# adaLN rows in the recurrent loop of a two-layer diffusion trunk: VectorE accumulation, or column groups on TensorE

## The chip, the cores and the metric

The kernel runs on one core of a Trainium2 chip. The engines of the core work side by side, each through its own queue in order: TensorE (PE; matmuls, with weight loads listed apart as PEld), VectorE (DVE), ScalarE (ACT), GpSimd (POOL) and SyncE (SP), which here issues the DMAs. The metric is the device time of one execution in microseconds.

## The reference

Two layers over 256 tokens of width 2048, float32. Each layer has a token mixer and a SwiGLU feed-forward, each behind an adaLN shift and scale and in front of a gated residual with LayerNorm. The first layer's mixer is a bidirectional gated linear recurrence (RG-LRU) over 2816 channels, started from 256 context tokens; the second is a pooling mixer.

```python
for i in range(DEPTH):
    m = jnp.split((cond_lat @ mod_w[i] + mod_b[i])[:, None, :], 6, axis=-1)
    h = x * (1 + m[1]) + m[0]
    ...
    y = mix(h)            # layer 0: RG-LRU, layer 1: pooling
    x = _layer_norm(ALPHA * x + m[2] * y, ln_g[i, 0], ln_b[i, 0])
    h = x * (1 + m[4]) + m[3]
    x = _layer_norm(ALPHA * x + m[5] * _swiglu(h, ffn_w1[i], ffn_w3[i], ffn_w2[i]), ln_g[i, 1], ln_b[i, 1])
```

In the recurrence, `a = exp(-8 r softplus(-lam))` and `b = sqrt(1 - a^2) * (i * xb)` with `r` and `i` sigmoids of block-diagonal products of `xb`, the output of a short convolution over `h @ w_x`. The state runs `h_t = a_t h_(t-1) + b_t` in both directions; the sum of both is multiplied by `gelu(h @ w_gate)` and projected by `w_out`.

What the change is about is `cond_lat @ mod_w[i]`: one row of 2048 numbers times a 2048 x 12288 matrix, in six vectors of 2048 for each layer, 16.8 MB of weights for each vector.

## The kernel before

**Weights.** All matrices stream from HBM once. A float32 weight piece (`raw`, four buffers) is split into a high half `hi` (a cast to the fast matmul format) and a low half `lo = raw - hi` (`split_w`, lines 183 to 192), and each product is three matmuls (`mm3`, lines 214 to 217): high x high, and the two mixed ones. The cast runs on ScalarE, or on GpSimd where `hi_pool` is set; the difference on VectorE, or on GpSimd where `lo_pool` is set. Buffers of `hi` and `lo` are three each.

**Jobs.** The program is a list of jobs. A `Runner` writes them out: loads go ahead as far as the limits of their class allow (`raw` 4, `mraw` 2), splits go up to two weight jobs ahead, uses (the matmuls) in order. `spread_mod` interleaves a second list, the adaLN jobs, into a main list. A scheduler then orders the instructions on each engine by dependence and by the place in this program.

**Stages.** In the first stage the shift and scale of layer 0 are computed while half of `h @ w_x` already runs; here the adaLN rows (`mu`, line 416) are multiplied on TensorE, 32 columns wide in four column groups. Then comes the recurrent loop over eight pairs of blocks (352 channels each). For each pair `p`:

- `wx_job`: `w_x` of the pair, two k-tiles a job, three jobs for the first five pairs (the rest of their sums was made in the first stage), eight for the last three; results in banks 0 to 2.
- `gates(p - 1, 1)`: two jobs of the `r` and `i` products of the pair before, backward direction, in banks 3 to 5; sigmoids on ScalarE.
- `conv(p)`: the convolution taps on VectorE, put at the head of the background list `bg`.
- `gate_job`: eight jobs of `h @ w_gate` with the tokens stationary, 352 columns wide, in banks 6 and 7, closed by a gelu (`gtok`, line 573).
- `gates(p, 0)`: two jobs, forward direction, then `recur`.

`recur` (line 619) queues the recurrence: tanh on ScalarE and `i * xb` on GpSimd at once (`f1`), then in the background exp (`f2`), square root (`f3`), two products on VectorE (`f4`), and the scans on VectorE (`f5`). After the loop come the projection by `w_out`, the first feed-forward, the pooling mixer, and the second feed-forward.

**adaLN on VectorE.** `mod_jobs` (line 220) takes half a vector at a time: 16 loads of 128 rows x 1024 columns (`mraw`), each followed by one VectorE instruction, `acc = mraw * cond + acc` (lines 246 and 249, 243 behind a fence). GpSimd then cuts the accumulator in two (lines 274 and 275), TensorE sums over the partitions by a matmul with ones (284 and 285), and the vector is brought into columns by way of DRAM (`finish_cols`) or added to a broadcast row (`finish_row`). Seven halves stand in the recurrent loop, 112 such instructions (vectors 3 and 4 of layer 0, half of vector 0 of layer 1, and vector 2 of layer 0, whose accumulators are kept until `row_now`); eleven halves run beside the projection and the first feed-forward, and two beside the second.

**GpSimd in the loop.** It makes the high half of six of each pair's eight `gate_job` pieces (`GH`) and of all `gates` pieces, the low half of four of the eight (`GL`), and `i * xb`. Later it adds the position embedding, makes the low halves of transposed activations (`jit`, line 766), and scales rows.

Of the kernel before, what the change touches and what calls it, by code (L numbers as in the profile page):

```python
# [10 lines left out]
F32 = mybir.dt.float32  # L11
F32R = mybir.dt.float32r
AF = mybir.ActivationFunctionType
ALU = mybir.AluOpType
# [18 lines left out]
LD = 0.85  # L33
# [5 lines left out]
GH = (1, 1, 1, 0)  # L39
GL = (0, 1, 0, 1)  # L40
# [21 lines left out]
class Runner:  # L62
    """Weights stream through SBUF in the order in which TensorE uses them."""
# [76 lines left out]
def trunk(es, tc, x, ctxlat, cols_in, ccols, mod_w, mod_b, ln_g, ln_b, ffn_w1, ffn_w3, ffn_w2,  # L140
# [23 lines left out]
    nc.scalar.activation(cond, craw[:, 0:KT], AF.Silu)  # L164
    mb01 = P.tile([128, 2, KT], F32, name="mb01")
# [4 lines left out]
    R = Runner({"raw": 4, "mraw": 2, "mu": 8, "xc": 2})  # L170
# [49 lines left out]
    def mod_jobs(vectors):  # L220
        """Products of the rows of mod_w with the conditioning vector, half a vector at a
        time; the sums over the partitions of one half run beside the next half's rows."""
        js = []
        wait = []
        for layer, which, finish, *halves in vectors:
            for h in halves or range(2):
# [31 lines left out]
                if finish is None:  # L258
                    st["acc", h] = acc
                else:  # L260
                    for n in range(1024 // MW):
                        wait += sums(layer, which, 1024 // MW * h + n, acc, n, finish)
# [47 lines left out]
    def row_now(layer, which):  # L310
        row = st["rows"].tile([128, D], F32, name="rowm", bufs=2)
        nc.sync.dma_start(row, mod_b[layer:layer + 1, which * D:(which + 1) * D].broadcast_to((128, D)))
        st["row", layer, which] = row
        for n in range(4):
            b = bk[st["rowbanks"][n % 2]]
            acc = st["acc", n // 2][0]
            nc.tensor.matmul(b, ones, acc[:, n % 2 * 512:(n % 2 + 1) * 512], start=True, stop=True)
            finish_row(layer, which, n, b, 512)

# [20 lines left out]
    cm = S_pool.tile([128, KT, 32], F32, name="cm")  # L340
# [33 lines left out]
    # startup: shift and scale of the first layer, two k-tiles at a time  # L374
# [184 lines left out]
    def gate_job(p, kt):  # L559
# [17 lines left out]
        return wjob(two_kt(rg_w_gate, kt * 128, p * PW, PW), 128, 2 * PW, use, hi_pool=GH[kt // 2 % 4], lo_pool=GL[kt // 2 % 4])  # L577
# [12 lines left out]
    def gates(p, d):  # L590
        def use(mat, j):
# [5 lines left out]
            for o, parts in enumerate((((0, 128, 0), (256, 128, 1)),  # L597
# [3 lines left out]
                b = bk[3 + o]  # L601
# [12 lines left out]
        for mat in range(2):  # L614
            js.append(wjob([(lambda r: r[:, :832], rg_wri[mat, d, p])], 128, 832,
                           lambda j, mat=mat: use(mat, j), hi_pool=True))
        return js

    def recur(p, d):
# [5 lines left out]
        def f1(t):  # L625
# [4 lines left out]
            nc.gpsimd.tensor_tensor(i[t][:m], i[t][:m], xb[t][:m], op=ALU.mult)  # L630
# [14 lines left out]
        def f5(t):  # L645
# [7 lines left out]
            else:  # L653
# [6 lines left out]
                z = st["pair"].tile([128, 256], F32, name="yg", bufs=3)  # L660
                nc.vector.tensor_tensor(z[:m], y, q["g"][t][:m], op=ALU.mult)
                row = 0
                while row < m:
                    k, o = divmod(p * PW + t * 128 + row, 128)
                    n = min(128 - o, m - row)
                    nc.sync.dma_start(U[o:o + n, k * 256:(k + 1) * 256], z[row:row + n])
# [8 lines left out]
    VL = [(0, 3, finish_cols), (0, 4, finish_cols), (1, 0, finish_cols, 0)]  # L675
    VF = [(0, 5, finish_row), (1, 0, finish_cols, 1), (1, 1, finish_cols),
# [92 lines left out]
    def project(w, nk, source, banks, which, aux, final=False):  # L769
        """[tokens, D] product in three column passes: 0:1024, 1024:1536, 1536:2048."""  # L770
# [11 lines left out]
        def wide(k):  # L782
# [173 lines left out]
    # first layer: project the gated recurrence, then feed forward  # L956
# [179 lines left out]
def _columns(rows):  # L1136
    """Rows of 128 become columns."""
# [15 lines left out]
def _fold(rows):  # L1153
    """[n, 1024] becomes [128, 8, n]: channel 128 a + p at [p, a]."""
# [3 lines left out]
def _bands():  # L1158
    """Window means over the tokens, and the identity."""
# [12 lines left out]
def _gate_blocks(w):  # L1172
    """[2, 16, 176, 176] blocks as zero-padded tiles [2, 8, 128, 832]."""
# [46 lines left out]
```

## Time and profile before

| | |
|---|---|
| timed runs | 2616.08, 2622.93, 2627.61 us; median 2622.93 |
| profiled execution | span 2613.2 us from its first to its last instruction; its own time with what lies around that isn't listed |
| stretch 0 to 192 us | first stage |
| stretch 192 to 836 us | recurrent loop |
| stretch 836 to 1640 us | projection and first feed-forward |
| DMA over the span | 597.19 MB, mean 229 GB/s |

The span is 2.9 us below the fastest timed run and 9.7 below the median. A row of a group reads: line, engine, operation, output<-inputs, shapes, count, then busy us and mean ns of one, then idle time of the engine just before such instructions and what ended it. A row of a wait reads: engine and line that waited, <-, engine and line that released it: us in total, times, longest. A matmul's length in the timeline overlaps the next one's, so its cost is read from the distance between starts. The float32 matmuls of lines 416 and 434 appear as two records each. TensorE's granted clock is given as a share of full speed.

### The profile page before, as it was taken

To read this page: it belongs to the slowest core of one execution; us is meant where nothing else is said; L and a number is where in the kernel's file an instruction comes from. 1 tells how busy PE (TensorE), PEld (TensorE's weight loads), DVE (VectorE), ACT (ScalarE), POOL (GpSimd) and SP (SyncE) were. 2 spreads that over 40 slices of the span, in tenths; PEclk is the share of its full clock that TensorE was granted. 3 is DMA by queue.
4 is the path that set the end of the run, shared out by engine and by line. 5 is a ranking of instruction groups with operands and counts; after the bars stand their busy time and mean duration, and the time that the engine had idled before them with its cause. 6 is when DMAs were issued, how large, how long until landed. Compare 5 with 4: busy or idle time off the path is not lost.

```text
span 2613.2 us, 29167 instructions
## 1 busy us (share of the span) xinstructions
PE 2373.4 (91%) x10336; PEld 1879.9 (72%) x10336; DVE 1850.5 (71%) x1866; ACT 1166.8 (45%) x1465; POOL 805.2 (31%) x485
## 2 busy tenths in 40 slices
PE   8998788799887889999999998897899999999997
PEld 4557666677765668787877776675677888888885
DVE  3559999978887978877767778649866444444565
ACT  3215556545564444444434444445433444444453
POOL 0004555543354461100001134855410000003366
PEclk9999898899998989999999999998899999999999
DMA  9876565566675859899988888654587666666664
GB/s 311 266 218 217 168 181 164 171 213 214 190 244 188 284 208 325 308 308 314 306 304 312 289 285 266 194 151 148 196 295 254 192 188 191 186 192 186 186 196 135
DMA packets 287539, 597.19 MB, mean 229 GB/s; under 512 B 33160, under 2 KB 101768, under 8 KB 285344
## 3 DMA queue, kind: packets, MB, share of 16 engines
q1 hardware_dynamic: 287392, 595.32, 71.0%
q8 instruction: 81, 1.33, 0.2%
q14 instruction: 66, 0.54, 0.1%
HBM read 590.21 MB, written 2.15 MB: 227 GB/s over the span
## 4 chain that ended last, share of the span: by engine, by line
PE 49%; DVE 21%; DMA 18%; issue 7%; POOL 2%; ACT 2%; SPq 1%; DVEq 0%; POOLq 0%; ACTq 0%
DMA mraw<-in_mod_w 15%; PE bank L217 15%; PE bank L216 15%; PE bank L215 15%; DVE lo L191 7%; DVE acc L249 4%; PE bank L416 2%; DVE th L643 1%; DVE th L642 1%; DVE xb L543 1%; DMA raw<-in_rg_w_out 1%; DVE xt L750 1%; DVE y L652 1%; DVE xt L735 1%; POOL jit L766 1%
## 5 line engine op out<-in xcount | busy, mean ns | idle before, releaser
L191 DVE TENSOR_TENSOR lo<-raw,hi 128x1024 fp32r<-128x1024 f32 (+2 forms) x700 | 892.2, 1282 | 418.8 <-ACT hi L189 388.3
L189 ACT CAST hi<-raw 128x1024 fp32r<-128x1024 f32 (+1 forms) x660 | 672.1, 1020 | 960.5 <-PE bank L216 827.1
L217 PE MATMUL bank<-lo,hh 128*128 128x512 f32 x1440 | 567.5, 394 | 16.5 <-DVE lo L191 16.3
L249 DVE SCALAR_TENSOR_TENSOR acc<-mraw,cond,acc 128x1024 f32<-128x1024 f32 x300 | 425.2, 1417 | 212.7 <-DMA mraw<-in_mod_w 211.5
L215 PE MATMUL bank<-hi,hh 128*128 128x512 f32 x1440 | 567.6, 395 | 5.8 <-ACT hh L1059 4.3
L216 PE MATMUL bank<-hi,hl 128*128 128x512 f32 x1440 | 566.0, 393 | 3.6 <-DVE hl L856 2.7
L217 PE MATMUL bank<-lo,jit 128*128 128x512 f32 x880 | 352.2, 401 | 31.9 <-DVE lo L191 30.2
L216 PE MATMUL bank<-hi,jit 128*128 128x512 f32 x880 | 350.1, 398 | 10.9 <-POOL jit L766 10.9
L215 PE MATMUL bank<-hi,jit 128*128 128x512 f32 x880 | 347.3, 395 | 2.0 <-ACT hi L189 2.0
L766 POOL TENSOR_TENSOR jit<-gT,jit 128x512 fp32r<-128x512 f32 x132 | 236.0, 1790 | 352.5 <-ACT jit L765 352.5
L217 PEld LDWEIGHTS bank<-lo,hh 128*128 128x128 f32 x1440 | 272.9, 190 | 81.1 <-DVE lo L191 24.3
L216 PEld LDWEIGHTS bank<-hi,hl 128*128 128x128 f32 x1440 | 273.0, 190 | 62.8 <-DVE hl L856 4.1
L215 PEld LDWEIGHTS bank<-hi,hh 128*128 128x128 f32 x1440 | 273.0, 190 | 62.1 <-ACT hh L1059 4.8
L274 POOL TENSOR_SCALAR mh<-acc 128x512 fp32r<-128x512 f32 x36 | 34.2, 949 | 804.1 <-PE bank L284 600.2
L217 PEld LDWEIGHTS bank<-lo,jit 128*128 128x128 f32 x880 | 167.9, 191 | 78.5 <-DVE lo L191 41.8
L216 PEld LDWEIGHTS bank<-hi,jit 128*128 128x128 f32 x880 | 167.5, 190 | 51.8 <-POOL jit L766 13.9
L215 PEld LDWEIGHTS bank<-hi,jit 128*128 128x128 f32 x880 | 167.8, 191 | 39.7 <-ACT hi L189 3.3
L216 PE MATMUL bank<-hTh,lo 128*128 128x512 f32 (+1 forms) x384 | 153.2, 400 | 0.0
L215 PE MATMUL bank<-hTh,hi 128*128 128x512 f32 (+1 forms) x384 | 150.5, 405 | 1.8 <-ACT hTh L446 1.8
L217 PE MATMUL bank<-hTl,hi 128*128 128x512 f32 (+1 forms) x384 | 151.6, 396 | 0.0
L217 PE MATMUL bank<-lo,hTh 128*128 128x352 f32 x256 | 94.5, 370 | 49.3 <-DVE lo L191 37.7
L630 POOL TENSOR_TENSOR i<-i,xb 128x512 f32<-128x512 f32 (+1 forms) x48 | 97.0, 2037 | 127.4 <-ACT i L606 127.3
(153 smaller groups left out, 2835.4 us busy)
## 6 DMA issues: line engine op xcount, KB each, us to landing
raw<-in_ffn_w SPq DMA_DIRECT2D x528, 512.0 KB
mraw<-in_mod_w SPq DMA_DIRECT2D x320, 512.0 KB
mu<-in_mod_w SPq DMA_DIRECT2D x128, 256.0 KB
raw<-in_rg_w_x SPq DMA_DIRECT2D x64, 352.0 KB
raw<-in_rg_w_gate SPq DMA_DIRECT2D x64, 352.0 KB
raw<-in_rg_w_out SPq DMA_DIRECT2D x44, 512.0 KB
raw<-in_rg_wri SPq DMA_DIRECT2D x32, 416.0 KB
xc<-in_ctxlat SPq DMA_DIRECT2D x8, 512.0 KB
```

Of the source, the lines that this page charges most:

```text
L189: nc.scalar.copy(hi[:k, :n], raw[:k, :n])
L191: e.tensor_tensor(lo[:k, :n], raw[:k, :n], hi[:k, :n].bitcast(F32), op=ALU.subtract)
L215: nc.tensor.matmul(bank, lh, rh, start=start, stop=False)
L216: nc.tensor.matmul(bank, ll, rh, start=False, stop=False)
L217: nc.tensor.matmul(bank, lh, rl, start=False, stop=stop)
L249: nc.vector.scalar_tensor_tensor(a, raw, c, a, op0=ALU.mult, op1=ALU.add)
L274: nc.gpsimd.tensor_scalar(mh, a, 1.0, 0.0, op0=ALU.mult, op1=ALU.add)
L416: nc.tensor.matmul(bk[6][32 * g:32 * g + 32, :], cm[:, kk, :], j.raw[:, a].rearrange("p m f -> p (m f)"), start=kk < 4, stop=kk >= 12)
L543: nc.vector.scalar_tensor_tensor(o3[:, :, od], u3[:, :, us], rgcol(w, p, t)[:m], o3[:, :, od], op0=ALU.mult, op1=ALU.add)
L630: nc.gpsimd.tensor_tensor(i[t][:m], i[t][:m], xb[t][:m], op=ALU.mult)
L642: nc.vector.scalar_tensor_tensor(th[t][:m], r[t][:m], 1.0, th[t][:m], op0=ALU.add, op1=ALU.mult)
L766: nc.gpsimd.tensor_tensor(lo, src, hi.bitcast(F32), op=ALU.subtract)
```

## The change

In the recurrent loop the adaLN products use the way of the first stage. `mod_chunk` takes a quarter of a vector (512 columns) in eight pieces of 256 rows; two pieces give four matmuls, one for each of the four column groups, accumulated over the 16 k-tiles in bank 5. ScalarE copies the bank; four small matmuls with the selector `selt` then sum the groups and turn the result into columns, and VectorE adds the bias from the bank. For vector 2 of layer 0 the copies are kept, and `row_now` sums them with `selr`. Four whole vectors stand in the loop now, the second half of vector 0 of layer 1 among them, which leaves the later stage. The pieces use two buffers of `mraw` and the three of `jit`. All casts and low halves of the loop go to ScalarE and VectorE, and so does `i * xb`, which VectorE does in `f2`. Because bank 5 is taken, `gates` uses banks 3, 4, 0, 1 or 3, 4, 6, 7. The adaLN jobs are spread evenly over the loop, `yg` is written in place, and the conditioning tile `cm` moves to the base pool.

```diff
-LD = 0.85
-GH = (1, 1, 1, 0)
-GL = (0, 1, 0, 1)
...
+    selr = P.tile([128, 128], F32, name="selr")
+    nc.vector.tensor_scalar(selr, ones, selt[:, 0:1], None, op0=ALU.mult)
...
-    R = Runner({"raw": 4, "mraw": 2, "mu": 8, "xc": 2})
+    R = Runner({"raw": 4, "mraw": 2, "mu": 8, "xc": 2, "mp": 5})
...
-            acc = st["acc", n // 2][0]
-            nc.tensor.matmul(b, ones, acc[:, n % 2 * 512:(n % 2 + 1) * 512], start=True, stop=True)
+            nc.tensor.matmul(b, selr, st["part", n], start=True, stop=True)
...
+    MBANK = 5
+    ring = ["mraw", "jit", "jit", "mraw", "jit"]
+    def mod_chunk(layer, which, n, keep):
...
+                name = ring[turn_mp[0] % len(ring)]
+                turn_mp[0] += 1
+                raw = P.tile([128, 1024], F32, name=name, bufs=3 if name == "jit" else 2)
+                nc.sync.dma_start(raw.rearrange("p (a f) -> p a f", a=2),
+                                  mod_w[layer, q * 256:(q + 1) * 256,
+                                        which * D + n * 512:which * D + (n + 1) * 512]
+                                  .rearrange("(a p) f -> p a f", p=128))
...
+                ready.append((q, j.raw))
+                if q % 2 == 0:
+                    return
+                for r, raw in ready:
+                    for a in range(2):
+                        kk = 2 * r + a
+                        g = kk % 4
+                        nc.tensor.matmul(bk[MBANK][32 * g:32 * g + 32, :], cm[:, kk, :],
+                                         raw[:, a * 512:(a + 1) * 512], start=kk < 4, stop=kk >= 12)
...
+            nc.scalar.copy(m, bk[MBANK])
...
+            for a in range(4):
+                nc.tensor.matmul(b[:, 2 * a:2 * a + 2], m[:, a * 128:(a + 1) * 128], selt, start=True, stop=True)
...
+            nc.vector.tensor_tensor(mcols[layer, which][:, 4 * n:4 * n + 4],
+                                    b[:, 0:8].rearrange("p (a s) -> p a s", s=2)[:, :, 0],
+                                    cols[:, o:o + 4], op=ALU.add)
...
-        return wjob(two_kt(rg_w_gate, kt * 128, p * PW, PW), 128, 2 * PW, use, hi_pool=GH[kt // 2 % 4], lo_pool=GL[kt // 2 % 4])
+        return wjob(two_kt(rg_w_gate, kt * 128, p * PW, PW), 128, 2 * PW, use)
...
+        if d == 0:
+            banks = (3, 4, 0, 1, 3, 4)
+        else:
+            banks = (3, 4, 6, 7, 3, 4) if p < PAIRS - 1 else (3, 4, 7, 3, 4, 7)
...
-                           lambda j, mat=mat: use(mat, j), hi_pool=True))
+                           lambda j, mat=mat: use(mat, j)))
...
-            nc.gpsimd.tensor_tensor(i[t][:m], i[t][:m], xb[t][:m], op=ALU.mult)
...
         def f2(t):
             m = ROWS[t]
+            nc.vector.tensor_tensor(i[t][:m], i[t][:m], xb[t][:m], op=ALU.mult)
...
-                return split_w(raw, 128, 1024, lo_pool=nk == DRNN // 128 and k in (4, 6)) + (pair[0],)
+                return split_w(raw, 128, 1024) + (pair[0],)
...
-    VL = [(0, 3, finish_cols), (0, 4, finish_cols), (1, 0, finish_cols, 0)]
-    VF = [(0, 5, finish_row), (1, 0, finish_cols, 1), (1, 1, finish_cols),
+    VF = [(0, 5, finish_row), (1, 1, finish_cols),
...
-    ml = mod_jobs(VL + [(0, 2, None)])
-    n5 = 16 * SPLIT - 3
-    loop = spread_mod(loop, ml, [(2, 0), (n5 - 2, LD), (len(loop) - n5, 1)])
+    ml = []
+    for layer, which in ((0, 3), (0, 4), (1, 0), (0, 2)):
+        for n in range(4):
+            ml += mod_chunk(layer, which, n, which == 2)
+    loop = spread_mod(loop, ml, [(len(loop), 1)])
```

On VectorE, at the end of a backward recurrence in one of the last three pairs (`i` and `y` hold the scan and its output), before:

```order
L655 SCALAR_TENSOR_TENSOR i<-r,th 96x256
L191 TENSOR_TENSOR lo<-raw,hi 128x704
L657 SCALAR_TENSOR_TENSOR i<-r,i,th 96x256
L249 SCALAR_TENSOR_TENSOR acc<-mraw,cond,acc 128x1024
L659 TENSOR_TENSOR y<-y,i 96x256
L249 SCALAR_TENSOR_TENSOR acc<-mraw,cond,acc 128x1024
L661 TENSOR_TENSOR yg<-y,gt 96x256
L191 TENSOR_TENSOR lo<-raw,hi 128x704
L249 SCALAR_TENSOR_TENSOR acc<-mraw,cond,acc 128x1024 x2
```

and of the change:

```order
L729 SCALAR_TENSOR_TENSOR i<-r,th 96x256
L190 TENSOR_TENSOR lo<-raw,hi 128x704
L731 SCALAR_TENSOR_TENSOR i<-r,i,th 96x256
L733 TENSOR_TENSOR y<-y,i 96x256
L734 TENSOR_TENSOR y<-y,gt 96x256
L190 TENSOR_TENSOR lo<-raw,hi 128x704
L707 TENSOR_TENSOR i<-i,xb 128x512 x2
L707 TENSOR_TENSOR i<-i,xb 96x512
```

The accumulations between the scans are gone; the products `i * xb` of the next recurrence, which were GpSimd's, stand behind them.

On TensorE, where the gate products of the second pair begin (`xh`, `xl` are the halves of `xb`; bank_66 is bank 5, bank_67 and bank_68 are banks 6 and 7), before:

```order
L215 MATMUL bank_67<-hi,hTh 128x352
L216 MATMUL bank_67<-hi,hTl 128x352
L217 MATMUL bank_67<-lo,hTh 128x352
L215 MATMUL bank_68<-hi,hTh 128x352
L216 MATMUL bank_68<-hi,hTl 128x352
L217 MATMUL bank_68<-lo,hTh 128x352
```

and of the change:

```order
L375 MATMUL bank_66<-selt,mh 128x2 x4
L214 MATMUL bank_67<-hi,hTh 128x352
L215 MATMUL bank_67<-hi,hTl 128x352
L216 MATMUL bank_67<-lo,hTh 128x352
L214 MATMUL bank_68<-hi,hTh 128x352
L215 MATMUL bank_68<-hi,hTl 128x352
L216 MATMUL bank_68<-lo,hTh 128x352
L348 MATMUL bank_66<-jit,cm 32x512 x4
```

Between the six gate matmuls of one k-tile and the next now stand the four column matmuls of one quarter vector, and behind them the first four row products of the next quarter, in the same bank.

On ScalarE, at the forward gates of an early pair (sigmoids `r`, transposed gelu `gt`, tanh `th`), before:

```order
L189 CAST hi<-raw 128x704
L606 ACT_TABLE_LOAD
L606 ACTIVATE r<-bank_64,cols 128x512
L587 COPY gt<-bank_67 128x256
L606 ACTIVATE r<-bank_65,cols 128x512
L587 COPY gt<-bank_68 128x256
L606 ACTIVATE r<-bank_66,cols 96x512
L189 CAST hi<-raw 128x704
```

and of the change:

```order
L188 CAST hi<-raw 128x704
L369 COPY ml<-bank_66 128x512
L680 ACT_TABLE_LOAD
L680 ACTIVATE r<-bank_64,cols 128x512
L656 COPY gt<-bank_67 128x256
L656 COPY gt<-bank_68 128x256
L680 ACTIVATE r<-bank_65,cols 128x512
L656 COPY gt<-bank_67 96x256
L703 ACTIVATE th<-r,cht 128x512
L680 ACTIVATE r<-bank_61,cols 96x512
```

The copy of bank 5 stands ahead of the sigmoids' table load, and the third `r` comes from bank 0 (bank_61) in place of bank 5.

More of the change, by code (lines that the diff above doesn't have):

```diff
@@ L257, in mod_jobs @@
                 assert not wait
[L258 to L262, printed above, removed]
+                for n in range(1024 // MW):
+                    wait += sums(layer, which, 1024 // MW * h + n, acc, n, finish)
         for w in wait:
@@ L315, in row_now, with piece, load, use @@
             b = bk[st["rowbanks"][n % 2]]
-            acc = st["acc", n // 2][0]
-            nc.tensor.matmul(b, ones, acc[:, n % 2 * 512:(n % 2 + 1) * 512], start=True, stop=True)
+            nc.tensor.matmul(b, selr, st["part", n], start=True, stop=True)
             finish_row(layer, which, n, b, 512)
+    MBANK = 5
+    ring = ["mraw", "jit", "jit", "mraw", "jit"]
+    turn_mp = [0]
+    def mod_chunk(layer, which, n, keep):
+        js = []
+        ready = []
+        out = {}
+        def piece(q):
+            j = Job()
+            j.cls = "mp"
+            def load():
+                name = ring[turn_mp[0] % len(ring)]
[5 more added lines that the diff above has]
+                                  .rearrange("(a p) f -> p a f", p=128))
+                return raw
+            def use(j):
+                ready.append((q, j.raw))
[7 more added lines that the diff above has]
+                                         raw[:, a * 512:(a + 1) * 512], start=kk < 4, stop=kk >= 12)
+                ready.clear()
+                R.free("mp")
+                R.free("mp")
+                if q == 7:
+                    keep_part()
+            j.load = load
+            j.use = use
+            return j
+        def keep_part():
+            if keep:
+                if n % 2 == 0:
+                    st["keep"] = P.tile([128, 1024], F32, name="acc", bufs=2)
+                m = st["keep"][:, n % 2 * 512:(n % 2 + 1) * 512]
+                st["part", n] = m
+            else:
+                m = P.tile([128, 512], F32, name="mh" if n % 2 else "ml")
+                out[0] = m
+            nc.scalar.copy(m, bk[MBANK])
+        def columns():
+            m = out[0]
+            b = bk[MBANK]
+            for a in range(4):
+                nc.tensor.matmul(b[:, 2 * a:2 * a + 2], m[:, a * 128:(a + 1) * 128], selt, start=True, stop=True)
+            if n == 0:
+                mcols[layer, which] = P.tile([128, KT], F32, name=f"mc{layer}{which}")
+            o = C_MODB + (layer * 6 + which) * KT + 4 * n
+            nc.vector.tensor_tensor(mcols[layer, which][:, 4 * n:4 * n + 4],
+                                    b[:, 0:8].rearrange("p (a s) -> p a s", s=2)[:, :, 0],
+                                    cols[:, o:o + 4], op=ALU.add)
+        js = [piece(q) for q in range(8)]
+        js.append(None)
+        if not keep:
+            js.append(plain(columns))
+        return js
@@ L339, in trunk @@
     S_pool = S_guard.__enter__()
-    cm = S_pool.tile([128, KT, 32], F32, name="cm")
+    cm = P.tile([128, KT, 32], F32, name="cm")
     nc.vector.memset(cm, 0.0)
@@ L590, in gates @@
     def gates(p, d):
+        if d == 0:
+            banks = (3, 4, 0, 1, 3, 4)
+        else:
+            banks = (3, 4, 6, 7, 3, 4) if p < PAIRS - 1 else (3, 4, 7, 3, 4, 7)
         def use(mat, j):
@@ L600, in use @@
                 m = ROWS[o]
-                b = bk[3 + o]
+                b = bk[banks[3 * mat + o]]
                 for n, (c, k, t) in enumerate(parts):
@@ L659, in f5 @@
                 nc.vector.tensor_tensor(y, y, h[:, 256:], op=ALU.add)
-                z = st["pair"].tile([128, 256], F32, name="yg", bufs=3)
-                nc.vector.tensor_tensor(z[:m], y, q["g"][t][:m], op=ALU.mult)
+                nc.vector.tensor_tensor(y, y, q["g"][t][:m], op=ALU.mult)
                 row = 0
@@ L665, in f5 @@
                     n = min(128 - o, m - row)
-                    nc.sync.dma_start(U[o:o + n, k * 256:(k + 1) * 256], z[row:row + n])
+                    nc.sync.dma_start(U[o:o + n, k * 256:(k + 1) * 256], y[row:row + n])
                     row += n
```

## The prediction

> **What bounds the kernel now.** I read the page first, then busy time by stage, then the waits of each engine inside the stage that the change touches.
>
> ```profile
> PE 2373.4 (91%) x10336; PEld 1879.9 (72%) x10336; DVE 1850.5 (71%) x1866; ACT 1166.8 (45%) x1465; POOL 805.2 (31%) x485
> ```
>
> The 91% says that TensorE is the bound, but it is a mean. The stages differ (from:to, length, busy us of PE, PEld, DVE, ACT and POOL with instructions, granted clock, DMA share, GB/s; the startup's steady part, the recurrent loop, the way through the first feed-forward):
>
> ```profile
> 65.00:192.00 127.00, 127.00 (x584) 73.93 (x583) 73.15 (x127) 24.91 (x38) 7.19 (x5) 1.00 0.77 242
> 192.00:836.00 644.00, 533.78 (x2337) 434.11 (x2335) 558.21 (x582) 351.61 (x488) 312.69 (x191) 0.90 0.63 193
> 836.00:1700.00 864.00, 803.25 (x3465) 645.76 (x3465) 665.45 (x578) 363.68 (x422) 240.12 (x143) 0.98 0.84 284
> ```
>
> In the loop (192 to 836) VectorE is busy 558 of 644 us, TensorE has 110 us idle and a clock of 0.90. How much work TensorE has there at full speed follows from the spacing of starts in two runs without a stop (28 rows from the first to the second, and 51 from the third to the fourth):
>
> ```profile
> 191.89 0.40 PE L217 MATMUL bank<-hTl,hi 128*128 128x512 f32 x1
> 198.16 0.39 PE L217 MATMUL bank<-hTl,hi 128*96 128x512 f32 x1
> 198.38 0.32 PE L215 MATMUL bank<-hi,hTh 128*128 128x352 f32 x1
> 206.40 0.32 PE L215 MATMUL bank<-hi,hTh 128*128 128x352 f32 x1
> ```
>
> 0.232 us for 512 columns, 0.160 for 352. The loop's 768 matmuls of 352 columns and some 1569 others make 123 + 364 = 487 us. So **157 of the 644 us are lost**, idle or at a low clock. What TensorE, ScalarE and VectorE waited for in the loop (waiter, releaser: us, times, longest):
>
> ```profile
> PE bank L217 <- DVE lo L191: 44.4, 14, 6.5
> PE bank L215 <- ACT r L606: 38.3, 10, 8.4
> PE bank L217 <- POOL lo L191: 12.9, 8, 2.8
> ...
> ACT xh L550 <- DVE xb L543: 67.2, 18, 7.0
> ACT L606 <- DVE y L652: 53.8, 5, 12.3
> ACT L606 <- DVE i L657: 40.2, 7, 7.8
> ...
> DVE acc L249 <- DMA mraw<-in_mod_w: 44.4, 40, 3.6
> ```
>
> TensorE waits for the low halves of weights that VectorE and GpSimd make late, and for ScalarE's sigmoids (r), which in turn wait for VectorE's scans. VectorE is late because it accumulates the adaLN rows, and stops in order for their DMAs. VectorE bounds the loop.
>
> **What is taken off VectorE and GpSimd.** Groups in the loop (busy us, mean ns | idle before), and last the low half in the stretch 8 to 192:
>
> ```profile
> L249 DVE SCALAR_TENSOR_TENSOR acc<-mraw,cond,acc 128x1024 f32<-128x1024 f32 x106 | 160.0, 1509 | 44.7 <-DMA mraw<-in_mod_w 44.4
> L191 DVE TENSOR_TENSOR lo<-raw,hi 128x704 fp32r<-128x704 f32 x68 | 83.1, 1223 | 3.9 <-ACT hi L189 3.2 <-POOL hi L187 0.7
> L643 DVE TENSOR_TENSOR th<-th,i 128x512 f32<-128x512 f32 x32 | 27.8, 881 | 0.0
> L191 POOL TENSOR_TENSOR lo<-raw,hi 128x704 fp32r<-128x704 f32 x32 | 74.5, 2327 | 26.3 <-ACT hi L189 18.2 <-DVE lo L191 4.2 <-PE bank L217 2.7
> L630 POOL TENSOR_TENSOR i<-i,xb 128x512 f32<-128x512 f32 x32 | 65.8, 2067 | 122.9 <-ACT i L606 122.9
> L187 POOL TENSOR_SCALAR hi<-raw 128x704 fp32r<-128x704 f32 x47 | 52.9, 1127 | 56.0 <-PE bank L217 42.8 <-PE bank L216 10.3 <-DVE lo L191 2.8
> L187 POOL TENSOR_SCALAR hi<-raw 128x832 fp32r<-128x832 f32 x32 | 36.8, 1156 | 44.3 <-PE bank L217 33.2 <-PE bank L216 9.2 <-POOL i L630 1.0
> L189 ACT CAST hi<-raw 128x704 fp32r<-128x704 f32 x52 | 40.3, 775 | 30.0 <-PE bank L217 25.3 <-PE bank L216 3.7 <-DMA raw<-in_rg_w_x 0.9
> L606 ACT ACT_TABLE_LOAD x25 | 32.1, 1283 | 94.3 <-DVE y L652 53.8 <-DVE i L657 40.2
> L191 DVE TENSOR_TENSOR lo<-raw,hi 128x704 fp32r<-128x704 f32 x28 | 25.6, 913 | 21.0 <-ACT hi L189 21.0
> ```
>
> VectorE loses about 160 us of accumulation and the 44 us of stops. It gains 32 low halves at 0.913 us (29) and 48 products i*xb at no more than 0.881 (42): 558 - 160 + 71 = 469 at most. The same low half takes 1223 ns beside a busy GpSimd and 913 in the stretch where GpSimd is nearly idle; 68 of those give 21 us back, and I take 60 for all two-input operations, an estimate: 409. That is 64% to 76% of a loop of 614 us; in the startup VectorE was 58% busy and TensorE lost nothing.
>
> The Trainium skill, page "SBUF — State Buffer", section "Who interferes with whom", says that a VectorE instruction with two SBUF inputs and a GpSimd instruction that reads SBUF exclude each other for the whole instruction. By that rule GpSimd leaving is worth more than its own work, as the two rows of the low half suggest; without it the 469 would stand, and I would give the slow rival below 0.30 and not 0.22. The sum itself doesn't use it.
>
> ScalarE gains 48 casts of 704 columns at 0.775 (37), 32 of 832 at about 0.92 (scaled by width; 29), 16 copies of a bank in place of ten short ones (about 4) and 8 table loads of 1.283 that the new order holds in addition (10): 352 + 80 = 432 us, 70% of 614. That is 54 us a pair, some 52 in the short pairs below, which have five casts fewer.
>
> **What TensorE gains.** The startup already computes such products in four column groups (L416), and the timeline shows visits of two and of six matmuls, each matmul being two records, then a group of four for the columns (L434):
>
> ```profile
> 62.20 0.39 PE L217 MATMUL bank<-hTl,hi 128*96 128x512 f32 x1
> 62.52 1.05 PE L416 MATMUL bank<-mu,cm 128*32 128x512 f32 x4
> 63.51 0.51 PE L215 MATMUL bank<-hTh,hi 128*128 128x512 f32 x1
> 63.85 0.40 PE L216 MATMUL bank<-hTh,lo 128*128 128x512 f32 x1
> ...
> 67.58 0.39 PE L217 MATMUL bank<-hTl,hi 128*96 128x512 f32 x1
> 67.90 1.91 PE L416 MATMUL bank<-mu,cm 128*32 128x512 f32 x12
> 69.74 0.97 PE L215 MATMUL bank<-hTh,hi 128*128 128x512 f32 x3
> 70.56 1.05 PE L434 MATMUL bank<-selt,ms 128*128 128x2 f32 x8
> 71.47 0.48 PE L216 MATMUL bank<-hTh,lo 128*128 128x512 f32 x1
> 71.79 0.40 PE L217 MATMUL bank<-hTl,hi 128*128 128x512 f32 x1
> ```
>
> Two matmuls push the next one back by 63.51 - 62.20 - 0.23 = 1.08 us, and its successor by another 0.11: 1.19. Six push by 69.74 - 67.58 - 0.23 = 1.93, with the 0.11 2.04. The 0.85 between is one more turn of the array (six go in two turns, so up to four run side by side), and 0.34 is what coming and going costs. A group of four in the changed loop is one turn: 64 x 1.19 = 76 us. The page "TensorEngine Tiling (Array Packing)" of the Trainium skill, section "Key Properties", states that a change of tiling mode drains TensorE, without a price. That speaks against 64 short visits; were both neighbours' full 0.39 us exposed, a visit would cost 0.85 + 0.78 and the 64 would cost 104 us, 28 more than by the 1.19, which is what the trace shows and what I use.
>
> Four column matmuls push by 0.93 + 0.09 = 1.02 us: 12 x 1.02 = 12. The 20 sums by ones go: -5. So **TensorE gets 83 us more work** in the stage that VectorE bounded: 570 of 644. The gain must come out of the 157 lost.
>
> **The sum, by pair.** The gelu that ends each pair's gate products (first, fifth, last pair):
>
> ```profile
> 223.71 0.95 ACT L573 ACTIVATE gtok<-bank 128x352 f32<-128x352 f32 x2 [2.85 <-PE bank L217]
> 499.20 0.82 ACT L573 ACTIVATE gtok<-bank 128x352 f32<-128x352 f32 x2
> 752.04 0.94 ACT L573 ACTIVATE gtok<-bank 128x352 f32<-128x352 f32 x2 [1.74 <-PE bank L217]
> ```
>
> Four short periods (3 of the jobs wx, 15 weight jobs in all) take 275.5 us, 68.9 each; their TensorE work is 138 x 0.232 + 96 x 0.160 = 48 us with the transposes. Three long ones (20 jobs) take 252.8, 84.3 each, for 69 us. So 21 and 15 us are lost in each. The additions, spread evenly over 141 jobs, are (76 + 12) / 141 = 0.63 us a job: work becomes 58 and 82. Of the loss I let 4 us a period stand: VectorE's lateness, GpSimd's 2.3 us products and the scans that held the sigmoids go; waits on ScalarE's casts and the new bank hand-offs come. Its bounds are 0 (the startup lost none) and the whole 21 and 15. Then short periods take 62 (4 x 62 - 275.5 = -27) and long ones 86 (3 x 86 - 252.8 = +5). The first 32 us gain 7 us of work and lose a stop on VectorE with its slow clock, 0. The last 84, where no rows are left to add, lose some 8 of their waits (8.4 on the sigmoids is the longest). Together **-30** in the loop.
>
> DMA doesn't bind: 128 pieces of 512 KB in place of 112 add 7% to the loop's 193 GB/s, where the next stage moves 284, and five buffers, three of them lent by jit, stand where two stood.
>
> After the loop 16 of 176 accumulations are gone:
>
> ```profile
> PE bank L217 <- DVE lo L191: 30.1, 26, 3.0
> ```
>
> That is TensorE's wait between 836 and 1640 us; a sixteenth to an eleventh of it makes -3 (nothing if the rest closes up, -30 if the 8.4 MB counted in full at 284 GB/s). In all -33. The span is 2613.2, 9.7 below the median of the timed runs, 2622.9; I put the same -33 on the median: **2590 us**.
>
> **Rivals.**
> - *ScalarE becomes the bound (slower).* Casts, sigmoids and table loads stand in one queue. Its waits for VectorE in the rows above are 161 us, 20 a pair; if they stay, a short pair needs 52 + 20 = 72 us and a long one loses 8: 288 and 270 us, +12 and +17, with the first stretch +4 and the tail unchanged +33, less 3: 2653. For it: ScalarE's own work is 90% of a short pair's TensorE work. Against it: those waits are for the engine that is relieved. It decides from a loss of 9 us a pair, at which the gain is nil.
> - *Bank 5 as a hand-off (same).* One bank takes every group of rows, then ScalarE copies it, TensorE takes columns into the same bank, VectorE adds them, and the next group must wait. 28 hand-offs at 1.2 us each are 33: 2623. For it: six matmuls of 0.16 stand between columns and the next group at the place shown. Against it: two such stops were hidden in the startup, where 0 was lost.
> - *TensorE alone bounds.* No loss in the pairs and 10 less in the tail: 28 + 10 more, 2552.
>
> **Chances.** Forecast (a loss of 1 to 7 us a pair, 2569 to 2611) 0.45, TensorE alone 0.13, hand-off 0.20, ScalarE 0.22. This kernel's runs can tell 0.5%, 13 us, from no change: faster 0.62, same 0.18, slower 0.20. The range takes in most of both far cases: 2548 to 2645.
>
> **What would show it.** In the changed profile the loop should end near 806 of the span, with VectorE under 470 us, ScalarE near 430, granted clock above 0.95, and TensorE's waits on VectorE's low half and on r under 30 together; a group of four near 1.2 us. Wrong it is if TensorE waits for ScalarE's casts or for bank 5's copy by more than 60 us, if a group pushes by more than 1.6 us, or if the stage after the loop changes by more than 10.

## The result and the profile after

The changed kernel takes **2545.65 us** (median of four, 2537.34 to 2549.30); the kernel before, timed beside it, 2619.51. The ratio is 0.972, with an interval of 0.968 to 0.976. That is 74 us less, where 33 were forecast, and 2.3 us under the low end of the range; one of the four runs lies inside it. The profiled execution agrees: its span went from 2613.2 to 2542.6 us, 70.6 less.

First the changed kernel's page (its first part), then its loop, and its first feed-forward from the first product with `hh` to the first with `band` (columns as ahead of the prediction):

```profile
PE 2400.2 (94%) x10920; PEld 1859.0 (73%) x10920; DVE 1663.7 (65%) x1830; ACT 1239.5 (49%) x1557; POOL 505.5 (20%) x299
...
192.00:784.00 592.00, 571.39 (x2919) 418.09 (x2918) 391.80 (x566) 424.31 (x581) 24.90 (x10) 0.98 0.67 224
...
897.00:1698.00 801.00, 761.12 (x3321) 618.00 (x3320) 578.34 (x504) 347.40 (x402) 213.38 (x128) 0.99 0.79 268
```

The loop is now a TensorE stage: 571 of 592 us busy, at a clock of 0.98 (before: 534 of 644, at 0.90). VectorE went from 558 to 392, ScalarE from 352 to 424. The waits inside it, of TensorE (all of them), ScalarE and VectorE (the longest):

```profile
PE bank L214 <- ACT r L680: 8.6, 1, 8.6
PE bank L216 <- DVE lo L190: 5.7, 2, 5.2
PE bank L214 <- ACT hi L188: 5.7, 2, 4.8
PE bank L215 <- POOL jit L840: 0.6, 1, 0.6
...
ACT hi L188 <- PE bank L216: 79.2, 25, 4.6
ACT hi L188 <- PE bank L215: 33.2, 23, 5.4
...
DVE lo L190 <- ACT hi L188: 97.4, 49, 5.8
```

TensorE waits 20.6 us in the whole loop, and 18.6 of them in three single stops of 8.6, 5.2 and 4.8. All of these lie behind the last gelu: from 192 us to its start at 697.68 TensorE is busy for the whole 505.68 us. ScalarE waits for TensorE to give back buffers, and VectorE waits for ScalarE: both are ahead of TensorE, the other way round from before. No wait on bank 5 is among them.

The same gelu starts that the prediction used:

```profile
219.15 0.95 ACT L642 ACTIVATE gtok<-bank 128x352 f32<-128x352 f32 x2 [0.61 <-PE bank L216]
450.88 0.94 ACT L642 ACTIVATE gtok<-bank 128x352 f32<-128x352 f32 x2 [0.60 <-PE bank L216]
697.68 0.82 ACT L642 ACTIVATE gtok<-bank 128x352 f32<-128x352 f32 x2
```

With them, and with the first products of the feed-forward and of the pooling mixer (in each row the duration's least, median and most, then first and last start), the span falls into stages; before, then after:

```profile
L215 PE MATMUL bank<-hi,hh x1440: 387/389/795, 945.7 to 2351.3; 128*128 128x512 f32 x180
...
L1042 PE MATMUL bank<-band,gT x64: 388/398/797, 1765.1 to 1815.9; 128*128 128x512 f32 x64
```
```profile
L214 PE MATMUL bank<-hi,hh x1440: 387/389/796, 897.4 to 2282.8; 128*128 128x512 f32 x180
...
L1116 PE MATMUL bank<-band,gT x64: 389/395/797, 1697.7 to 1748.4; 128*128 128x512 f32 x64
```

| stage | before | after | change | forecast |
|---|---|---|---|---|
| to the first gelu | 223.7 | 219.2 | -4.6 | 0 |
| four short periods | 275.5 | 231.7 | -43.8 | -27 |
| three long periods | 252.8 | 246.8 | -6.0 | +5 |
| last gelu to first feed-forward | 193.7 | 199.7 | +6.1 | -8 |
| first feed-forward | 819.4 | 800.3 | -19.1 | -3 |
| rest | 848.1 | 844.9 | -3.2 | 0 |
| sum | 2613.2 | 2542.6 | -70.6 | -33 |

A short period takes 57.9 us where I had 58 of work and 62 in all, a long one 82.3 where I had 82 and 86. So two things are to be explained: that nothing was lost in the pairs, and the 19 us of the feed-forward.

### The profile page after: what moved, and what is told of

It reads as the page before. It is cut to its first block, busy times and chain, and to the rows that moved or that the text cites. A ratio compares the mean times of both kernels' runs of the same rounds, so it can differ in the third digit from the quotient of the medians.

```text
span 2542.6 us, 30010 instructions
## 1 busy us (share of the span) xinstructions
PE 2400.2 (94%) x10920; PEld 1859.0 (73%) x10920; DVE 1663.7 (65%) x1830; ACT 1239.5 (49%) x1557; POOL 505.5 (20%) x299
## 4 chain that ended last, share of the span: by engine, by line
PE 71%; DMA 12%; DVE 10%; issue 3%; ACT 2%; POOL 1%; SPq 1%; DVEq 0%; POOLq 0%; ACTq 0%
PE bank L214 22%; PE bank L216 21%; PE bank L215 21%; DMA mraw<-in_mod_w 10%; DVE lo L190 4%; PE bank L348 2%; PE bank L485 2%; DVE acc L248 1%; DVE xt L824 1%; POOL jit L840 1%; DVE xt L809 1%; PE bank L956 1%; SPq L201 1%; DMA mu<-in_mod_w 0%; ACT hi L188 0%
## 5 line engine op out<-in xcount | busy, mean ns | idle before, releaser
L188 ACT CAST hi<-raw 128x1024 fp32r<-128x1024 f32 (+2 forms) x740 | 737.4, 998 | 1015.4 <-PE bank L215 855.7
L216 PE MATMUL bank<-lo,hh 128*128 128x512 f32 x1440 | 566.2, 393 | 12.8 <-DVE lo L190 12.6
L248 DVE SCALAR_TENSOR_TENSOR acc<-mraw,cond,acc 128x1024 f32<-128x1024 f32 x180 | 238.1, 1323 | 150.6 <-DMA mraw<-in_mod_w 149.8
L840 POOL TENSOR_TENSOR jit<-u,jit 128x512 fp32r<-128x512 f32 x33 | 56.1, 1706 | 651.7 <-DMA raw<-in_rg_w_out 553.2
L270 POOL TENSOR_SCALAR mh<-acc 128x512 fp32r<-128x512 f32 x24 | 20.7, 864 | 794.0 <-PE bank L280 575.3
L214 PEld LDWEIGHTS bank<-hTh,hi 128*128 128x128 f32 (+1 forms) x384 | 68.1, 180 | 51.9 <-issue 15.9
```

The lines of the kernel that those rows point to most:

```text
L188: nc.scalar.copy(hi[:k, :n], raw[:k, :n])
L214: nc.tensor.matmul(bank, lh, rh, start=start, stop=False)
L216: nc.tensor.matmul(bank, lh, rl, start=False, stop=stop)
L248: nc.vector.scalar_tensor_tensor(a, raw, c, a, op0=ALU.mult, op1=ALU.add)
L840: nc.gpsimd.tensor_tensor(lo, src, hi.bitcast(F32), op=ALU.subtract)
```

## Experiments

Each kernel was timed beside the kernel before. "Loop end" is the start of the first product with `hh` (loop and projection together), "feed-forward" the stretch from there to the first product with `band`.

| kernel | loop end | feed-forward | time, us | ratio to before |
|---|---|---|---|---|
| before | 945.7 | 819.4 | 2619.51 | 1 |
| the change | 897.4 | 800.3 | 2545.65 | 0.972 (0.968 to 0.976) |
| e1 GpSimd back | 920.8 | 800.3 | 2570.10 | 0.982 (0.979 to 0.984) |
| e2 GpSimd out only | 898.0 | 820.4 | 2568.60 | 0.982 (0.979 to 0.984) |
| e3 half back | 883.4 | 820.1 | 2550.78 | 0.974 (0.972 to 0.976) |
| e4 groups of two | 944.4 | 803.1 | 2591.86 | 0.990 (0.988 to 0.992) |
| e5 one more vector | 913.2 | 791.3 | 2549.69 | 0.974 (0.972 to 0.976) |
| e6 groups of eight | 886.3 | 807.9 | 2535.75 | 0.969 (0.966 to 0.972) |
| e7 vector 2 on VectorE | 883.5 | 802.9 | 2529.83 | 0.967 (0.964 to 0.969) |
| e8 split and one more | 897.2 | 789.5 | 2540.49 | 0.971 (0.968 to 0.974) |
| e9 idle GpSimd products | 973.7 | 827.6 | 2651.25 | 1.013 (1.009 to 1.017) |
| e10 half, loads only | 880.3 | 817.0 | 2543.36 | 0.971 (0.968 to 0.974) |
| e11 half, work only | 891.5 | 803.6 | 2551.19 | 0.975 (0.972 to 0.979) |
| e12 ScalarE doubled | 906.9 | 802.7 | 2550.22 | 0.974 (0.971 to 0.977) |

A feed-forward with the changed kernel's work took 800.3 to 807.9 in the six kernels that have it (the change, e1, e4, e6, e7, e12; mean 802.9), so differences of a few us between single stages say nothing.

### Which half of the change won the loop

The change has two halves that can be taken apart: rows to TensorE, and GpSimd's work to ScalarE and VectorE. e1 keeps only the first, e2 only the second.

```diff
 e1, from the changed kernel
-        return wjob(two_kt(rg_w_gate, kt * 128, p * PW, PW), 128, 2 * PW, use)
+        return wjob(two_kt(rg_w_gate, kt * 128, p * PW, PW), 128, 2 * PW, use, hi_pool=GH[kt // 2 % 4], lo_pool=GL[kt // 2 % 4])
...
-                           lambda j, mat=mat: use(mat, j)))
+                           lambda j, mat=mat: use(mat, j), hi_pool=True))
...
+            nc.gpsimd.tensor_tensor(i[t][:m], i[t][:m], xb[t][:m], op=ALU.mult)
...
-            nc.vector.tensor_tensor(i[t][:m], i[t][:m], xb[t][:m], op=ALU.mult)
...
-                return split_w(raw, 128, 1024) + (pair[0],)
+                return split_w(raw, 128, 1024, lo_pool=nk == DRNN // 128 and k in (4, 6)) + (pair[0],)
 e2, from the kernel before: the same lines the other way round
```

> The changed kernel with GpSimd's work put back: its share of the casts and low halves in the loop and i*xb. Only the adaLN rows stay on TensorE. Theory (VectorE's accumulation was the whole loss, and TensorE now has nothing to wait for): VectorE is under 430 us in the loop, the loop grows by 0 to 10 us (GpSimd's low halves of 2.3 us come late a few times), time 2546 to 2556. Rival (GpSimd's slow products and its contention with VectorE made half of the loss): the loop grows by 25 us or more, time above 2570.

> The kernel before with only GpSimd's work of the loop moved to ScalarE and VectorE; the rows stay on VectorE. Theory (VectorE bounds by its accumulation): VectorE gains some 57 us of work and loses some 60 to contention, stays above 530 us in the loop and keeps bounding it; time 2605 to 2635, a gain of less than 15 us or a small loss. Rival (GpSimd's part was half of the loss): 2590 or less.

Both missed their theory, each in the direction of its rival: 2570 and 2569. e1 stands at the edge of that rival, e2 well inside it. In e2 the loop end is 898.0, as early as with the whole change, though VectorE still accumulates every row. The loop of e2, VectorE's waits in it, and two of its groups:

```profile
192.00:781.00 589.00, 515.21 (x2330) 414.88 (x2328) 520.19 (x666) 411.83 (x568) 73.26 (x30) 0.94 0.68 213
...
DVE acc L249 <- DMA mraw<-in_mod_w: 37.2, 37, 2.7
DVE i L633 <- ACT i L606: 10.5, 7, 3.3
DVE lo L191 <- ACT hi L189: 10.3, 10, 2.0
...
L249 DVE SCALAR_TENSOR_TENSOR acc<-mraw,cond,acc 128x1024 f32<-128x1024 f32 x108 | 139.1, 1288 | 37.4 <-DMA mraw<-in_mod_w 37.2
L191 DVE TENSOR_TENSOR lo<-raw,hi 128x704 fp32r<-128x704 f32 x99 | 86.8, 880 | 2.5 <-ACT hi L189 2.5
```

VectorE is busy 520 us and waits in these rows for 58: 578 of 589. It still bounds this loop. It took over 31 low halves (31 x 0.88 = 27 us) and 48 products (34 us, groups of 22.8 and 10.9), and yet was 38 us less busy than before: 558 + 61 - 520 = **99 us** went because its own instructions became shorter. An accumulation fell from 1509 to 1288 ns, the low half from 1223 to 880.

Was it GpSimd running beside VectorE, or GpSimd's slow results? e9 gives GpSimd work that nobody uses:

```diff
 e9, from e2
         e.tensor_tensor(lo[:k, :n], raw[:k, :n], hi[:k, :n].bitcast(F32), op=ALU.subtract)
+        if n in (2 * PW, 832) and "pair" in st:
+            nc.gpsimd.tensor_tensor(idle, hi[:, :512].bitcast(F32), hi[:, :512].bitcast(F32), op=ALU.mult)
```

> The kernel of e2_gpsimd_out_only with 131 products on GpSimd in the loop that nobody uses (hi x hi, 512 columns, into a tile of its own). GpSimd is busy some 250 us again, but nobody waits for its results. Theory (GpSimd beside VectorE slows VectorE's own instructions, and VectorE bounds that loop): VectorE's accumulation goes back to 1.45 us or more and its 704-column low half to 1.1 or more, the loop grows by 40 us or more, time above 2610. Rival (it was GpSimd's results that came late, 2.3 us for a low half): VectorE's durations stay and the time is 2565 to 2580.

2651 us: slower than the kernel before. GpSimd's group, VectorE's two, and ScalarE's wait for GpSimd:

```profile
L194 POOL TENSOR_TENSOR idle<-hi 128x512 bf16<-128x512 f32 x132 | 262.7, 1990 | 297.2 <-ACT hi L190 293.3
```
```profile
L252 DVE SCALAR_TENSOR_TENSOR acc<-mraw,cond,acc 128x1024 f32<-128x1024 f32 x106 | 150.9, 1424 | 29.9 <-DMA mraw<-in_mod_w 29.5
L192 DVE TENSOR_TENSOR lo<-raw,hi 128x704 fp32r<-128x704 f32 x99 | 100.2, 1015 | 3.6 <-ACT hi L190 3.6
```
```profile
ACT hi L190 <- POOL idle L194: 14.4, 7, 4.8
```

The accumulation rose by 136 ns and the low half by 135, a little less than expected, and the loop end by 75.7 us, more than expected. One side effect is in it: `hi` isn't free until GpSimd has read it, and ScalarE waited 14.4 us for that. But the lengthening is enough by itself: from 192 us to the loop end VectorE is busy 616 us in e2 (753 instructions) and 703 in e9 (754), which is 86 us more. So lateness isn't needed: GpSimd at work beside VectorE is enough to give back the whole 48 us and more.

The single instructions say the same. Of the 106 accumulations in the loop before, 63 overlap in time with a GpSimd instruction on tensors and take 1670 ns on average; the other 43 take 1274, and none of them over 1287. In e9 the means are 1525 ns for 60 that overlap and 1275 for 45 that don't, and for the low half of 704 columns 1077 (69) and 873 (30). The addition `u<-bank,u`, which has one of its two inputs in a bank, takes 674 ns with an overlap and 678 without. The Trainium skill, page "SBUF — State Buffer", section "Who interferes with whom", whose rule the prediction weighed, is borne out here: the products read SBUF and nobody used them, and VectorE's instructions with two SBUF inputs became longer, the two groups above by 11 and 15% on average and the convolution taps (128x510) from 741 to 1224 ns. That one engine stands still for the whole instruction of the other was not shown separately.

So the loop had two cures, and they don't add up. At the loop end the rows' move alone (e1) wins 24.9 us, GpSimd's leaving alone (e2) 47.7, and both together 48.3. With GpSimd out VectorE needs 589 us for the loop; with the rows moved as well TensorE needs 592, and half a vector more is done in them. At equal work, e3 below against e2, the rows' move is still worth 14.6 us at the loop end and 18 us of time; the changed kernel spends this on the half vector that it takes into the loop.

### Whether TensorE is the bound now, and what a visit costs

```diff
 e4, from the changed kernel: a piece is used as soon as it comes
-                if q % 2 == 0:
-                    return
...
-                R.free("mp")
                 R.free("mp")
 e6: four pieces at once, two buffers of acc lent for the first three vectors
-                if q % 2 == 0:
+                if q % 4 != 3:
 e12, in split_w: each cast of the loop twice
             nc.scalar.copy(hi[:k, :n], raw[:k, :n])
+            if n in (2 * PW, 832) and "pair" in st:
+                nc.scalar.copy(hi[:k, :n], raw[:k, :n])
```

> The changed kernel with 128 visits of two row products in place of 64 visits of four; the same 256 matmuls. If two cost as much as four (one turn of 0.85 us and 0.34 for coming and going, 1.19) and TensorE bounds the loop without slack, the loop grows by 64 x 1.19 = 76 us: 2618 to 2626. If TensorE had 4 us a period to spare, as the forecast had it, 30 us of these are hidden: 2585 to 2600. If two cost half of four, nothing changes: 2546.

> The changed kernel with 32 visits of eight row products in place of 64 visits of four (seven buffers in place of five for the first three vectors). If a visit costs 0.34 for coming and going and 0.85 for each turn of four, as the startup's visits of two and six showed, the loop loses 64 x 1.19 - 32 x 2.04 = 11 us: 2535. If the loads come late now, since four buffers are freed at once, TensorE waits for the row pieces and nothing is gained: 2546 or above.

> The changed kernel with every cast of a 704- or 832-column weight piece in the loop made twice on ScalarE (131 x 0.8 = 105 us more; ScalarE some 530 us of 592). Theory (ScalarE at 424 of 592 is far from the bound, its time is waits for buffers that TensorE frees): the loop grows by less than 10 us, time 2546 to 2556. Rival (ScalarE's queue is at the edge, as the slow rival of the prediction had it): TensorE waits for hi and r, the loop grows by 30 us or more, time above 2576.

TensorE's timeline around one visit: four products in the changed kernel, two in e4, eight in e6 (two records each):

```profile
329.67 0.32 PE L216 MATMUL bank<-lo,hTh 128*128 128x352 f32 x1
329.92 1.06 PE L348 MATMUL bank<-jit,cm 128*32 128x512 f32 x8
330.92 0.43 PE L214 MATMUL bank<-hi,hTh 128*128 128x352 f32 x1
331.18 0.32 PE L215 MATMUL bank<-hi,hTl 128*128 128x352 f32 x1
```
```profile
341.97 0.32 PE L216 MATMUL bank<-lo,hTh 128*128 128x352 f32 x1
342.23 1.05 PE L346 MATMUL bank<-mraw,cm 128*32 128x512 f32 x4
343.21 0.43 PE L214 MATMUL bank<-hi,hTh 128*128 128x352 f32 x1
343.47 0.33 PE L215 MATMUL bank<-hi,hTl 128*128 128x352 f32 x1
```
```profile
331.98 0.32 PE L216 MATMUL bank<-lo,hTh 128*128 128x352 f32 x1
332.24 1.07 PE L352 MATMUL bank<-jit,cm 128*32 128x512 f32 x8
...
334.09 0.51 PE L214 MATMUL bank<-xh,hi 128*128 128x512 f32 x1
334.43 0.40 PE L215 MATMUL bank<-xh,lo 128*128 128x512 f32 x1
```

Four push the next matmul by 330.92 - 329.67 - 0.16 = 1.09 us and its successor by 0.10: **1.19**. Two push by 1.08 + 0.10 = 1.18, as much as four. Eight push by 1.95 + 0.11 = 2.06. The prediction's split into 0.34 for coming and going and 0.85 a turn holds at all three sizes.

e4 came out at 2592, inside what I had expected if TensorE had 4 us a period to spare. That reading falls, since my count was wrong: where two pieces stand next to each other in the job list their visits join, and TensorE's order has 109 visits there, not 128, against 65 in the changed kernel. 44 x 1.18 = 52 us were added, and the loop end moved by 47. So nearly all of it came through. e6 took 31 long visits and three short ones, and gained 11.1 us at the loop end, as expected. e12 put 104 us more of casts on ScalarE. Its busy time in the loop rose by only 66 us of them, from 424 of 592 to 490 of 602, because 20 table loads fewer were needed in that order. The loop end moved by 9.5 us and the time by 5: ScalarE isn't the bound.

### Where the feed-forward's 19 us are from

```diff
 e3, from the changed kernel
-        for n in range(4):
+        for n in range(2 if layer else 4):
             ml += mod_chunk(layer, which, n, which == 2)
...
-    VF = [(0, 5, finish_row), (1, 1, finish_cols),
+    VF = [(0, 5, finish_row), (1, 0, finish_half, 1), (1, 1, finish_cols),
 e10, from e3, for that half only
+    s = slice(0, 8)
+    nc.vector.scalar_tensor_tensor(a[:, s], raw[:, s], c, a[:, s], op0=ALU.mult, op1=ALU.add)
 e11, from the changed kernel, for half of vector 1 of layer 1
     nc.vector.scalar_tensor_tensor(a, raw, c, a, op0=ALU.mult, op1=ALU.add)
+    nc.vector.scalar_tensor_tensor(a, raw, zcol, a, op0=ALU.mult, op1=ALU.add)
 e5, from the changed kernel
-    VF = [(0, 5, finish_row), (1, 1, finish_cols),
+    VF = [(0, 5, finish_row),
...
-    for layer, which in ((0, 3), (0, 4), (1, 0), (0, 2)):
+    for layer, which in ((0, 3), (0, 4), (1, 0), (1, 1), (0, 2)):
```

> The changed kernel with the second half of vector 0 of layer 1 back beside the projection and the first feed-forward, as 16 accumulations on VectorE; the loop loses two quarters (8 groups of four and 8 small matmuls). Theory (the feed-forward gained 19 us because these 16 accumulations left it, over 1 us each): the loop is 12 us shorter, the first feed-forward 15 to 20 longer, time 2549 to 2554. Rival (the feed-forward gained for another reason: the projection's low halves off GpSimd, or the way in which it is entered): the feed-forward changes by less than 5, time 2534 to 2539.

> The kernel of e3_half_back with the 15 later accumulations of the half that is back cut to 8 columns: its 8.4 MB are loaded all the same, VectorE's work on them (15 x 1.3 = 20 us) is gone. It leaves most of the sums for the second half of vector 0 of layer 1 undone. Theory (the first feed-forward is short of DMA while the adaLN rows load beside the weights): it stays at 817 to 822 us, time 2548 to 2553. Rival (VectorE's instructions delay the low halves): it falls to 800 to 805, time 2532 to 2537.

> The changed kernel with 15 accumulations more on VectorE beside the first feed-forward, on pieces of vector 1 of layer 1 that are loaded anyway (times zero, so that nothing changes in the result): VectorE's work of half a vector without its loads. Theory (DMA): the first feed-forward stays at 798 to 804 us, time 2544 to 2549. Rival (VectorE): it grows by 15 to 20 us, time 2560 to 2567.

> The changed kernel with a whole further vector, 1 of layer 1, taken out of the first feed-forward (32 accumulations on VectorE) into the loop's row products on TensorE (16 groups of four, 16 small matmuls). Theory (in the loop TensorE alone bounds, at 1.2 us a group and 1.0 for four columns; in the feed-forward an accumulation costs 1.2 us): loop + 16 x 1.2 + 4 x 1.0 = +23, feed-forward - 32 x 1.2 = -38, time 2530. Rival (the feed-forward's gain ends with the first half vector, since TensorE's own work there is near): feed-forward less than 10 shorter, time 2560.

e3: with the half back the feed-forward takes 820.1, as before the change, and in e2, which has the half there too, 820.4. So the 19 us belong to the half vector. Its loads without its VectorE work give 817.0, which is 9 to 17 us above the six kernels without the half. Its VectorE work without its loads gives 803.6, inside their spread. So it is mostly the **loads**. The whole times missed what I had written, e10 by 5 us below and e11 by 2 above; the stage itself came as the theory said in both.

One stretch of 200 us in the middle of the stage, before and after the change, and two waits of the whole stage, ScalarE's for weights and TensorE's for low halves, before and after:

```profile
1150.00:1350.00 200.00, 192.82 (x859) 157.65 (x860) 150.23 (x136) 80.44 (x86) 14.93 (x12) 1.00 0.90 304
...
ACT hi L189 <- DMA raw<-in_ffn_w: 26.9, 11, 8.5
PE bank L217 <- DVE lo L191: 22.3, 20, 2.6
```
```profile
1100.00:1300.00 200.00, 198.31 (x890) 162.99 (x889) 149.56 (x133) 83.56 (x89) 14.12 (x12) 1.00 0.87 303
...
PE bank L216 <- DVE lo L190: 11.7, 15, 2.6
...
ACT hi L188 <- DMA raw<-in_ffn_w: 6.5, 3, 2.8
```

The DMA moves 304 and 303 GB/s in the two, so the rate didn't change, but of these bytes fewer are adaLN rows (45 pieces in place of 49): TensorE gets through 890 matmuls in place of 859.

How the loads cost time is less clear. ScalarE's wait for weights doesn't follow the stage's length: it is 17.3 us in e10, 6.5 to 18.7 in the six kernels without the half, and 28.4 in e5, whose feed-forward is shorter than theirs. TensorE's wait for low halves does follow it: 22.3 us before, 23.1 in e2, 23.9 in e3, 19.8 in e10, but 10.0 in e11 and 11.7 to 14.0 in the six. VectorE makes the low halves, and in its own queue it stops for the row pieces, 136 us in this stage before, 156 in e10 and 109 after. e10 has these stops too. So whether the loads cost by the DMA's rate or by VectorE's stops for them ahead of the low halves was not taken apart.

e5 takes 16.8 MB more out and gains only 9.0 us, not 38 (its rival's number for the stage), with 255 GB/s on average. What it costs in the loop (15.8 us at the loop end) eats that, and its time, 2549.69, is neither the theory's nor the rival's.

### A split of the rows

```diff
 e7, from the changed kernel
-    ring = ["mraw", "jit", "jit", "mraw", "jit"]
+    ring = ["jit"]
...
-    for layer, which in ((0, 3), (0, 4), (1, 0), (0, 2)):
+    for layer, which in ((0, 3), (0, 4), (1, 0)):
...
     loop = spread_mod(loop, ml, [(len(loop), 1)])
+    loop = spread_mod(loop, mod_jobs([(0, 2, None)]), [(len(loop), 1)])
 e8, from e7: (0, 4, finish_cols) too goes to mod_jobs, (1, 1) from VF to mod_chunk
```

> The changed kernel with vector 2 of layer 0 back on VectorE in the loop (32 accumulations, kept as before for the row sums), the other three vectors on TensorE with the three jit buffers; GpSimd stays out. Theory (alone, VectorE without GpSimd and TensorE with all rows each need some 590 us for the loop, and a split of the rows needs less): TensorE loses 16 x 1.2 = 19 us of work and VectorE, at 392 + 32 x 1.3 = 433 and some 12 of stops, isn't the bound; time 2525 to 2530. Rival (VectorE's accumulations and their DMA stops hold up low halves, however idle VectorE is): TensorE's waits for lo come back, time 2546 or above.

> GpSimd out of the loop; there vectors 4 and 2 of layer 0 on VectorE (64 accumulations) and vector 3 of layer 0 and 0 and 1 of layer 1 on TensorE (48 groups of four); vector 1 of layer 1 leaves the feed-forward. Theory: in the loop TensorE loses 19 us of work, VectorE is at 392 + 64 x 1.3 = 475 and some 25 of stops, below TensorE's; feed-forward -38; time 2490. Rival (VectorE late in the loop again): loop as in the changed kernel, time 2508 or above.

If each engine alone needs some 590 us, a split should need less. e7's loop:

```profile
192.00:766.50 574.50, 554.80 (x2776) 413.48 (x2775) 421.49 (x593) 411.40 (x568) 22.21 (x10) 0.99 0.70 229
...
PE bank L216 <- DVE lo L190: 12.2, 3, 7.4
PE bank L352 <- DMA jit<-in_mod_w: 3.0, 4, 1.8
```

**2529.83 us, the fastest version**: its slowest run (2534.67) is below the changed kernel's fastest. The loop end moved by 13.9 us of the 19 expected; TensorE's wait for low halves, 5.7 us in the changed kernel, is 12.2 here. e6, with all rows on TensorE in long visits, is only 6 us slower, and its runs (2532.07 to 2538.83) overlap with e7's. e8 didn't do what was expected of it: its loop end is 897.2, as with the change, although TensorE has a quarter of the row products fewer there, and its feed-forward gained 10.8 us of the 38. In its loop VectorE was busy 462 of 593 us, and the loads ran at 249 GB/s. TensorE waited there 12.6 us for low halves and 6.1 for row pieces; what held it up beyond that was not settled.

## Why the prediction was right and wrong

- **Mechanism: right for the end, incomplete for the start.** VectorE bounded the loop, and now TensorE does. But VectorE was as long as it was because GpSimd ran beside it: e2 reaches the same loop end with every accumulation still in place. The prediction had 60 us for the relief of the operations that stay. The changed kernel shows at least 77 (469 less the 392 measured), and e2, where the accumulations count as well, 99. That this alone would do wasn't seen.
- **"Of the loss I let 4 us a period stand": the first step that failed.** It measured 0 (57.9 and 82.3 us for 58 and 82 of work). Seven periods at 4 us are 28, and the short and long periods together are 27.8 better than forecast. I had the lower bound, 0, from the startup, and chose against it for fear of ScalarE's casts and bank 5. Up to the last gelu TensorE doesn't stop at all, e12 shows ScalarE with room for 66 us more of work, and e4 that work added to TensorE comes through.
- **"A sixteenth to an eleventh of it makes -3": the second.** The half vector gave 19. I scaled TensorE's wait for low halves by the share of accumulations that left. That wait fell by half (22.3 to 11.7 us in the feed-forward) when one of eleven halves left, so it doesn't go by their number. The price is mostly that of the loads (9 to 17 us in e10), whose bound of -30 I had, from 8.4 MB at 284 GB/s, and kept only as the far end.
- **The tail's -8: wrong, with the other sign.** From the last gelu to the feed-forward it is +6.1. The wait on the sigmoid is still there (8.6 against 8.4), as nothing in the last recurrence was removed, and one visit of row products still stands there (at 709.07 us), where I had none left. Most of the rest lies behind the recurrence, up to the first feed-forward (107.7 us before, 112.9 after); no run took it apart.
- **The price of TensorE's new work: right.** 1.19 us for a group of four, as worked out from the startup. The forecast of 82 us of work a long period and 58 a short one came out within 0.3 us. Two slips change no term: 409 of 614 is 67% and not 64%, and (76 + 12) / 141 is 0.62 and not 0.63.
- **Rivals.** "TensorE alone bounds", with a chance of 0.13, is what happened in the pairs; its 2552 took 18 us off the tail, which grew by 6, and 3 off the feed-forward, which lost 19; that these nearly cancel is luck. ScalarE as the bound is refuted by e12, and bank 5 as a hand-off left TensorE no wait.
- **Signs.** VectorE under 470 (392), ScalarE near 430 (424), clock above 0.95 (0.98), waits on `lo` and `r` under 30 (14.3) all came; the loop ended earlier than 806. The warning that a change of over 10 us behind the loop would prove the prediction wrong came true.

## What to carry to other kernels

When an engine is the bound, look at how long its own instructions take beside an idle and beside a busy neighbour before moving its work: here taking GpSimd's share off the loop, which gave VectorE more instructions to do, was worth 48 us at the loop end, and taking VectorE's largest job away alone 25. When work leaves a stage, price its loads as well as its instructions, and don't scale a wait by the number of instructions that leave. And once TensorE becomes the bound, count its work from the spacing of starts: here the sum without an allowance was the right one. A split of the rows between the two engines then was the fastest version, a little ahead of long visits on TensorE alone.

## What the runs showed of the hardware

- 263 us of GpSimd products that nobody used made the loop end 76 us later where VectorE was the bound (e9). There an accumulation took 1525 ns when it overlapped with a GpSimd instruction and 1275 when it didn't, a low half 1077 and 873.
- Two, four and eight column-group matmuls between ordinary ones cost 1.18, 1.19 and 2.06 us: a pair costs as much as a full turn of four.
- With weights and adaLN rows loading together the DMA stayed at 303 to 304 GB/s whether 859 or 890 matmuls ran in the 200 us; in this stage 8.4 MB of loads, with VectorE's stops for them, cost 9 to 17 us (e10).
